# A decoder trunk in split float32: the down projection by seven block products instead of eight, and a scheduler that prices a port conflict

## The chip, the cores and the metric

The kernel runs on one core of one Trainium2 chip. Engines are named as in the profile: PE is TensorE (matmul), PEld its weight load, DVE is VectorE, ACT is ScalarE, POOL is GpSimd, SP is SyncE, which issues the DMAs. The metric is the device time of one execution in microseconds (us), lower being better.

## The reference

Two layers over 512 tokens of width 1024, all in float32. Each layer has a mixing part (four groups of attention heads that share an input projection and an output projection), then a squared-ReLU MLP, then a gated embedding added to the residual. The part that matters here:

```python
h = rmsnorm(x, g_pre_mlp)
m = jnp.square(jax.nn.relu(h @ w_up)) @ w_down   # 512x1024 @ 1024x4096, 512x4096 @ 4096x1024
x = x + rmsnorm(m, g_post_mlp)
x = x + jax.nn.sigmoid(x @ w_ple_gate) * (p_i @ w_ple_proj)
```

## The kernel before

**Arithmetic.** Every float32 operand of a large product is split into a high part `hi`, rounded to the type fp32r, and a rest `lo = x - hi`. `mm3` (L466) makes one product of 128 x 128 by 128 x 512 out of three matmuls: hi by hi, hi by lo, lo by hi. A split is one copy (`copy_r`, L461: ScalarE or VectorE) and one subtraction (`split`, L473: VectorE, or GpSimd where no operand lies in PSUM). Weights come by `wload` (L448): a DMA of 512 KB into a tile `wst` (2 buffers), then the split into `whi` and `wlo` (5 buffers each).

**Order of work.** The kernel is first recorded as a list of operations and then ordered by a planner (`schedule`, L290). It simulates the five engines with a price for each operation (`price`, L246) and a delay for each handover between engines (`SEEN`, L113), and takes on each engine the ready operation that was recorded first. The order that comes out is fixed: each engine runs its list in order. Operations recorded with `either` may go to one of two engines; `sooner_elsewhere` (L399) drops an engine if the operation would end sooner on the other, after adding a bias per engine (`plan.bias`). A buffer of a tag is handed out in the order of recording, to the next tile of the tag once all readers of an older one are done. The planner lets VectorE and GpSimd work side by side at full speed.

**The MLP** (`layer`, L1040). `up_tile(f)` (L1115) makes one of 32 tiles of the hidden activations, 128 hidden units by 512 tokens: 24 matmuls (8 steps of depth by 3) into a bank `ps_sc`, relu on ScalarE, a multiplication of that by the bank on VectorE, and the split into two scratch tiles. `down(g)` (L1130) multiplies 8 of these tiles by their weights through `token_major` (L1193): for each half of the 1024 columns four `wload` tiles and four banks (two `ps_mm`, two `ps_tp`), one for each 128 tokens, 192 matmuls in all. The four results are drained, the first group by a copy and the others by an addition to the accumulators `y`. In the fourth group the drained tile is also squared and summed, multiplied by a gain, normed, added to `x`, transposed on TensorE and split into `hT` for the gate product that follows. The loop is

```python
for g in range(5):
    for f in range(8):
        if g < 4:
            up_tile(8 * g + f)
        if g and f == 1:
            down(g - 1)
```

so that up tiles and down groups alternate on TensorE. A layer's MLP has 768 matmuls in the up and 768 in the down projection, each of 512 columns. `scratch` (L1187) takes its tiles in rotation from 20 buffers of the tags V, R and P0; the tag Z has 6 buffers, two of which hold the post gain during the MLP. PSUM has 8 banks: two `ps_mm`, two `ps_tp`, four `ps_sc`.

Of the kernel before, what the change touches and what calls it, by code (L numbers as in the profile page):

```python
# [134 lines left out]
class Plan:  # L135
# [110 lines left out]
    def price(self, eng, fn, a, k, outs, ins):  # L246
# [25 lines left out]
            return (470.0 if k.get("op") == ALU.pow else n * 2.1 + 147), 0.0  # L272
        return n * 0.833 + 244, 0.0

    @contextmanager
    def after(self, i):

        old, self.held = self.held, i
        yield
        self.held = old  # L280
# [9 lines left out]
    def schedule(self):  # L290
# [8 lines left out]
        now = dict.fromkeys(engines, 0.0)  # L299
        future = {e: [] for e in engines}  # L300
        avail = {e: [] for e in engines}
        dma, now["SP"] = 0.0, 560.0
        table = None
        waiting, live, last, queue = {}, {}, {}, {}

        def push(i):
            for e, r in ops[i].ready.items():
# [34 lines left out]
        while True:  # L342
            best = None
            for e in engines:
                f, v = future[e], avail[e]
                while f and (f[0][0] <= now[e] or ops[f[0][2]].done):
                    _, p, i = heapq.heappop(f)
                    heapq.heappush(v, (p, i))
                while v and ops[v[0][1]].done:
                    heapq.heappop(v)  # L350
                s = now[e] if v else f[0][0] if f else None
                if s is not None and (best is None or s < best[0]):
                    best = (s, e)
            if best is None:
                break
            s, e = best
            now[e] = max(now[e], s)
            f, v = future[e], avail[e]
            while f and f[0][0] <= s:
                _, p, i = heapq.heappop(f)  # L360
                heapq.heappush(v, (p, i))
            _, i = heapq.heappop(v)
            o = ops[i]
            if o.done or self.sooner_elsewhere(o, e, s, now, avail):
                continue
            o.start, o.done = s, True
            if o.alts:
                o.eng = e
                o.fn, o.a, o.k, o.cost, o.size = o.open[e]
            cost = o.cost  # L370
            if e == "PE" and s < COLD:
                cost *= 2
            if e == "ACT" and o.table and o.table != table:
                cost, table = cost + 1283, o.table
            now[e] = s + cost
            if e == "SP":
                dma = max(dma, s + cost + 650) + o.size
                o.end = dma
            else:
                o.end = now[e]  # L380
            order.append(i)
            for j in o.succ:
                q = ops[j]
                q.left -= 1
                after(q, e, o.end)
                if q.left == 0:
                    push(j)
            for t in o.tiles:
# [7 lines left out]
        self.total = max(o.end for o in ops)  # L396
        return order

    def sooner_elsewhere(self, o, e, s, now, avail):  # L399
        if not o.open or len(o.open) < 2:  # L400
            return False
        best = None
        for g, c in o.open.items():
            t = s if g == e else max(now[g], o.ready[g])
            if g != e:
                t += sum(self.ops[i].cost for p, i in avail[g] if p < o.prio and not self.ops[i].done
                         and not self.ops[i].alts)
            t += c[3] + o.bias.get(g, 0.0)
            if best is None or t < best[0]:
                best = (t, g)  # L410
        if best[1] != e:
            del o.open[e]
            del o.ready[e]
            return True
        return False
# [25 lines left out]
class Builder:  # L441
# [6 lines left out]
    def wload(self, src, S):  # L448

        nc = self.nc  # L450
        st = self.tile([128, 1024], F32, "wst")
        nc.sync.dma_start(st[:, :S], src)
        hi = self.tile([128, 1024], F32R, "whi")
        lo = self.tile([128, 1024], F32R, "wlo")
        s, h, l = st[:, :S], hi[:, :S], lo[:, :S]
        self.copy_r(h, s)
        self.plan.either(("vector", "tensor_tensor", (l, s, h.bitcast(F32)), dict(op=ALU.subtract)),
                         ("gpsimd", "tensor_tensor", (l, s, h.bitcast(F32)), dict(op=ALU.subtract)))
        return hi, lo

    def copy_r(self, out, src):  # L461

# [577 lines left out]
    def layer(self, L, x, last):  # L1040
        nc, t = self.nc, self.t
# [6 lines left out]
        with self.plan.shift(self.ple_shift):  # L1048
# [57 lines left out]
        self.token_major(lambda half, i: t["wo"][L, half, self.mixed[i]], [2 * g + k for g in self.mixed for k in (0, 1)],  # L1106
                         lambda k: (self.mixh[:, k, :], self.mixl[:, k, :]), evac_w, done_w, (False, True), part)

        self.plan.bias = {"DVE": self.mlp_bias}

        gpost2 = self.gain(t["g4"][L])
        xT = None
        uts = {}

        def up_tile(f):  # L1115
            wh, wl = self.wload(t["wu"][L, f], 1024)
            ps = self.tile([128, T], F32, "ps_sc")
            cs = (slice(0, 256), slice(256, 512)) if f < self.cut else (slice(0, 512),)
            for c in cs:
                for k in range(8):  # L1120
                    ks = slice(k * 128, (k + 1) * 128)
                    self.mm3(ps[:, c], wh[:, ks], wl[:, ks], hT[0][:, k, c], hT[1][:, k, c],
                             k == 0 and c == cs[0], k == 7 and c == cs[-1])
            r = self.tile([128, T], F32, "Z")
            nc.scalar.activation(r, ps, AF.Relu)
            nc.vector.tensor_tensor(r, r, ps, op=ALU.mult)
            uts[f] = (self.scratch(), self.scratch())
            self.split(*uts[f], r, sbuf=True)

        def down(g):  # L1130
            def evac_d(half, tt, ps):
                o = y[tt][half]
                if g == 0:
                    self.copy_r(o, ps)
                else:
                    nc.vector.tensor_tensor(o, ps, o, op=ALU.add)
                if g == 3:
                    self.square_half(ss2[tt], o, half, eps4[tt])
                    self.plan.either(*[(e, "tensor_tensor", (o, o, gpost2[half]), dict(op=ALU.mult))
                                       for e in ("gpsimd", "vector")])  # L1140

            def done_d(tt):
                nonlocal xT
                if g == 3:
                    if xT is None:
                        xT = self.new_hT()
                    self.add_normed(ss2[tt], y[tt], x[tt])
                    for i in range(2):
                        self.to_hT(x[tt][i], i, tt, xT)

            self.token_major(lambda half, i: t["wd"][L, g, half, i], range(8),
                             lambda k: uts[8 * g + k], evac_d, done_d, (False, g == 3))

        ss2 = [self.tile([128, 4], F32, "ss4") for tt in range(4)]
        for g in range(5):
            for f in range(8):
                if g < 4:
                    up_tile(8 * g + f)
                if g and f == 1:
                    down(g - 1)  # L1160


        self.plan.bias = {"DVE": 0.0 if last else self.mlp_bias}
# [23 lines left out]
    def scratch(self, dt=F32R):  # L1187

        self.unit += 1
        tags = ("V",) * 10 + ("R",) * 6 + ("P0",) * self.bufs[1]  # L1190
        return self.tile([128, T], dt, tags[self.unit * 7 % len(tags)])

    def token_major(self, src, korder, parts, evac, done, outer, part={}, fine=False):  # L1193
# [73 lines left out]
    first = ("v", "g", "v", "vg", "vg", "vg", "g", "g")  # L1267
    warm = 28

    parted = (0,)  # L1270
    part_tags = ("R", "V")

# [27 lines left out]
def _layout(inp):  # L1300

    f = lambda n: np.ascontiguousarray(np.asarray(inp[n]))
    w = f("w_in")
# [30 lines left out]
    a["wo"] = hv(f("w_out"), 2)  # L1334
    wu = f("w_mlp_up")
    a["wu"] = np.concatenate([chunks(wu[:, :, i * 128:(i + 1) * 128], 8) for i in range(32)], axis=1)
    wd = f("w_mlp_down").reshape(DEPTH, 4, 1024, D)
    a["wd"] = np.stack([hv(wd[:, g], 2) for g in range(4)], axis=1)
    a["wg"] = hv(f("w_ple_gate"), 2)
    a["wp"] = hv(f("w_ple_proj"), 2)[:, :, 0]  # L1340
    a["bf"] = f("b_forget")
# [26 lines left out]
```

## Time and profile before

| | us |
|---|---|
| median of 3 runs | 1509.18 (1507.07 to 1511.28) |
| the profiled execution, its own time | 1507.25 |
| its span, first to last instruction | 1505.5 |
| PE busy | 1445.8 (96%) |
| DVE busy | 908.8 (60%) |
| ACT busy | 661.1 (44%) |
| POOL busy | 376.7 (25%) |
| granted TensorE clock, mean over the span | 0.987 |

The time of the execution is 1.75 us more than its span. Busy time of PE is modelled: a matmul of 512 columns is listed with some 390 ns, and the next starts before that is over, so PE can be busy throughout and still have its pace set by the distance between starts. In time the kernel falls into mixing of layer 0 (to about 345 us), its MLP (to about 725), mixing of layer 1 (to about 1095) and its MLP (to about 1460); the gate product ends each layer.

### The profile page before, as it was taken

What the parts mean: (1) busy time and instruction counts of PE and PEld (TensorE: products, weight loads), DVE (VectorE), ACT (ScalarE), POOL (GpSimd) and SP (SyncE); (2) the same over time, 40 slices, a digit from 0 to 9 for tenths busy, and PEclk for the clock granted to TensorE, in tenths of its full rate; (3) what the DMA queues carried; (4) which work ended last, traced back from release to release, by engine and by line L of the source; (5) the groups of instructions that cost most, each with busy time, mean ns of one, the idle gap of its engine ahead of it and who ended that gap; (6) DMA issues with size and microseconds to landing.
All of it is one profiled execution on the core that took longest, in us unless ns stands there. A gap on an engine that the chain in (4) does not pass through costs nothing. (4 is left out here: it accounts for less than half of the span.)

```text
span 1505.5 us, 19889 instructions
## 1 busy us (share of the span) xinstructions
PE 1445.8 (96%) x7476; PEld 1173.3 (78%) x7476; DVE 908.8 (60%) x1789; ACT 661.1 (44%) x1299; POOL 376.7 (25%) x291
## 2 busy tenths in 40 slices
PE   6999998999999999999999999889999999999998
PEld 6967776778888888887789678577788888888877
DVE  7689998756424333335666999986553243433463
ACT  4266656745323223233344665666543341322321
POOL 5564556342000000002145636563310000000020
PEclk8899999999999999999999999999999999999999
DMA  4321122223222222221332211123132222222221
GB/s 160 100 86 57 57 78 98 78 84 112 99 90 93 98 98 88 94 98 56 122 118 71 74 55 64 64 64 120 52 131 98 99 88 94 98 98 90 92 77 63
DMA packets 44624, 133.91 MB, mean 89 GB/s; under 512 B 6896, under 2 KB 8176, under 8 KB 44528
## 3 DMA queue, kind: packets, MB, share of 16 engines
q1 hardware_dynamic: 44528, 132.64, 26.7%
q8 instruction: 59, 0.97, 0.3%
q14 instruction: 37, 0.30, 0.1%
HBM read 127.38 MB, written 5.24 MB: 88 GB/s over the span
## 5 line engine op out<-in xcount | busy, mean ns | idle before, releaser
L429 DVE TENSOR_TENSOR wlo<-wst,whi 128x1024 fp32r<-128x1024 f32 x150 | 184.2, 1228 | 355.6 <-ACT whi L429 355.4
L429 ACT ACTIVATE whi<-wst 128x1024 fp32r<-128x1024 f32 (+1 forms) x212 | 222.7, 1051 | 397.0 <-PE ps_tp L429 202.1
L429 POOL TENSOR_TENSOR wlo<-wst,whi 128x1024 fp32r<-128x1024 f32 (+1 forms) x70 | 168.5, 2410 | 164.2 <-ACT whi L429 155.8
L429 PE MATMUL ps_sc<-htl,whi 128*128 128x512 f32 (+1 forms) x544 | 208.5, 384 | 1.1 <-DVE htl L429 1.1
L429 PE MATMUL ps_sc<-hth,whi 128*128 128x512 f32 (+1 forms) x544 | 207.6, 383 | 0.3 <-ACT hth L429 0.3
L429 PE MATMUL ps_sc<-hth,wlo 128*128 128x512 f32 (+1 forms) x544 | 206.5, 380 | 0.0
L429 POOL TENSOR_SCALAR ss<-ss,eps 128x1 f32<-128x1 f32 x8 | 3.7, 473 | 637.1 <-ACT Z L429 637.1
L429 PE MATMUL ps_mm<-hth,whi 128*128 128x512 f32 (+1 forms) x400 | 148.3, 372 | 9.6 <-DVE R L429 9.2
L429 PE MATMUL ps_mm<-htl,whi 128*128 128x512 f32 (+1 forms) x400 | 148.1, 371 | 1.8 <-DVE htl L429 1.8
L429 PE MATMUL ps_mm<-hth,wlo 128*128 128x512 f32 (+1 forms) x400 | 146.2, 366 | 0.0
L429 PE MATMUL ps_mm<-whi,htl 128*128 128x512 f32 (+2 forms) x344 | 121.1, 353 | 5.6 <-DVE htl L429 5.6
L429 PE MATMUL ps_mm<-whi,hth 128*128 128x512 f32 (+2 forms) x344 | 122.0, 355 | 0.3 <-DVE V L429 0.2
L429 PE MATMUL ps_mm<-wlo,hth 128*128 128x512 f32 (+2 forms) x344 | 120.1, 350 | 0.1
L429 PEld LDWEIGHTS ps_sc<-hth,whi 128*128 128x128 f32 x544 | 102.0, 188 | 23.0 <-ACT hth L429 0.5
L429 PEld LDWEIGHTS ps_sc<-htl,whi 128*128 128x128 f32 x544 | 102.2, 188 | 22.4 <-DVE htl L429 1.5
L429 PEld LDWEIGHTS ps_sc<-hth,wlo 128*128 128x128 f32 x544 | 102.3, 188 | 21.9
L429 ACT ACTIVATE Z<-Z,m 128x256 f32<-128x256 f32 (+3 forms) x160 | 86.2, 541 | 39.4 <-DVE m L429 38.7
L429 PE MATMUL ps_tp<-whi,V 128*128 128x512 f32 x256 | 96.4, 394 | 0.0
L429 PE MATMUL ps_mm<-whi,V 128*128 128x512 f32 x256 | 96.4, 394 | 0.0
L429 PEld LDWEIGHTS ps_mm<-hth,whi 128*128 128x128 f32 x400 | 77.8, 195 | 20.6 <-issue 11.5
L429 POOL TENSOR_TENSOR R<-R,R 128x512 fp32r<-128x512 f32 (+1 forms) x58 | 76.6, 1321 | 59.1 <-ACT R L429 46.0
L429 PEld LDWEIGHTS ps_mm<-htl,whi 128*128 128x128 f32 x400 | 78.0, 195 | 13.1 <-issue 3.0
(213 smaller groups left out, 2957.4 us busy)
## 6 DMA issues: line engine op xcount, KB each, us to landing
wst<-in_wu SPq DMA_DIRECT2D x64, 512.0 KB, 3.2
wst<-in_wd SPq DMA_DIRECT2D x64, 512.0 KB, 3.2
wst<-in_wq SPq DMA_DIRECT2D x40, 512.0 KB, 3.5
wst<-in_wo SPq DMA_DIRECT2D x16, 512.0 KB, 3.3
wst<-in_wg SPq DMA_DIRECT2D x16, 512.0 KB, 3.2
R<-in_x SPq DMA_DIRECT2D x16, 256.0 KB, 3.6
Z<-in_g SPq DMA_DIRECT2D x16, 256.0 KB, 3.6
wst<-in_wv SPq DMA_DIRECT2D x8, 512.0 KB, 3.2
```

What stands on the lines that cost most here:

```text
L429: r = getattr(getattr(nc, eng), fn)(*[res(v) for v in o.a], **{n: res(v) for n, v in o.k.items()})
```

## The change

The down projection of the first 24 of the 32 hidden tiles is taken in 4 groups (`groups = 4`) of 3 pairs of tiles. A pair is a depth of 2 x 128; with two halves of the tokens (256 each) and two halves of the columns (512 each), it is a product of 2 x 2 by 2 x 2 blocks. Seven block products stand for the eight, with sums and differences of blocks on both sides (`sums` for the activations, the first loop of `down` and its second for the weights), and sums of the products over all pairs kept in `acc` and combined once (`blocks`). The last 8 tiles go the old way (`down_rest`).

```diff
-            r = self.tile([128, T], F32, "Z")
+            r = us[f] = self.tile([128, T], F32, "Z")
             nc.scalar.activation(r, ps, AF.Relu)
-            nc.vector.tensor_tensor(r, r, ps, op=ALU.mult)
-            uts[f] = (self.scratch(), self.scratch())
-            self.split(*uts[f], r, sbuf=True)
+            nc.scalar.activation(r, r, AF.Square)
+            if f >= 6 * self.groups:
+                uts[f] = (self.scratch(), self.scratch())
+                self.split(*uts[f], r, sbuf=True)
+            elif f % 2:
+                sums(f // 2)
+        def sums(p):
+            a, b = us.pop(2 * p), us.pop(2 * p + 1)
+            z = self.tile([128, T], F32, "Z")
+            y4 = self.tile([128, 256], F32, "Z")
+            self.either(ALU.add, z[:, lt], a[:, rt], b[:, rt])
+            self.either(ALU.subtract, z[:, rt], z[:, lt], a[:, lt])
+            self.either(ALU.subtract, a[:, rt], a[:, lt], a[:, rt])
+            self.either(ALU.subtract, y4, b[:, lt], z[:, rt])
+            for src, left, right in ((a, 1, 7), (z, 5, 6), (b, 2, 4), (y4, 3, None)):
...
         def down(g):
+            pairs = range(3 * g, 3 * g + 3)
+            banks = {n: [self.tile([128, T], F32, tag) for i in range(2)]
+                     for n, tag in (("x", "ps_mm"), ("y", "ps_tp"), ("v", "ps_sc"), ("w", "ps_sc"))}
+            for p in pairs:
+                a = self.tile([128, 1024], F32, "wst")
+                b22, t1 = self.scratch(F32), self.scratch(F32)
+                t2 = T2[p] = self.scratch(F32)
+                nc.sync.dma_start(a, t["wd"][L, 2 * p])
+                nc.sync.dma_start(b22, t["wd"][L, 2 * p + 1, :, 512:])
+                self.either(ALU.subtract, t1, a[:, w2], a[:, w1])
+                self.either(ALU.subtract, t2, b22, t1)
+                self.either(ALU.subtract, a[:, w2], b22, a[:, w2])
+                h, l = self.wparts()
+                self.split(h, l, a, sbuf=True)
+                B[p, 1], B[p, 7] = (h[:, w1], l[:, w1]), (h[:, w2], l[:, w2])
+                h, l = self.wparts()
+                for src, w, i in ((t1, w1, 5), (t2, w2, 6)):
+                    self.split(h[:, w], l[:, w], src, sbuf=True)
...
+            for p in pairs:
+                for n, bank in ((1, "x"), (5, "v"), (7, "w"), (6, "y")):
+                    for i in range(2):
+                        product(p, n, bank, i, p == pairs[0], p == pairs[-1])
+            for n, bank in ((1, "x"), (5, "v"), (7, "w"), (6, "y")):
+                for i in range(2):
+                    add(acc[n][i], banks[bank][i], g == 0)
+            for p in pairs:
+                c = self.tile([128, 1024], F32, "wst")
+                nc.sync.dma_start(c, t["wd"][L, 2 * p + 1])
+                self.either(ALU.subtract, T2[p], c[:, w1], T2[p])
...             # split of c for products 2 and 3, split of T2 for product 4,
...             # products 2 (bank x), 3 (v), 4 (w) of the three pairs, drained like the first four
+        def blocks():
+            for i in range(2):
+                a = {n: acc[n][i] for n in acc}
+                for o, b in ((2, 1), (6, 1), (5, 6), (3, 5), (5, 7), (4, 7), (4, 6)):
+                    self.either(ALU.add, a[o], a[o], a[b])
+        for f in range(32):
+            up_tile(f)
+            if f and f % 6 == 0 and f <= 6 * self.groups:
+                down(f // 6 - 1)
+                if f == 6 * self.groups:
+                    blocks()
+        down_rest()
```

In `down_rest` the multiplication by the gain goes to VectorE alone, where the planner chose before. The biases of the MLP up to there become 1000 ns for VectorE and 4000 ns for GpSimd (before: 500 and 0). `scratch` rotates over 29 buffers: 10 of V, 11 of R, 4 of P0 and the 4 of `tab`, which hold the rope tables during the mixing. The numbers of buffers of each tag stay.

The planner gets a model of a port that VectorE and GpSimd share. It acts on the whole kernel, not on the MLP alone:

```diff
+    def shared(self, fn, a):
+        ins = [v for v in a[1:] if isinstance(v, View) and v.free() > 64]
+        if any(self.psum(v) for v in a if isinstance(v, View)):
+            return False
+        return len(ins) > 1 or fn[1] in ("tensor_copy", "tensor_scalar")
...
+            if e == "DVE" and self.shared(o.fn, o.a):
+                cost += max(0.0, port["POOL"] - s)
+                port["DVE"] = s + cost
+            if e == "POOL":
+                cost += max(0.0, port["DVE"] - s)
+                port["POOL"] = s + cost
```

`sooner_elsewhere` counts the same: an engine that would have to wait for the port is priced from the time when the port comes free.

## Rows read from the trace of the kernel before

**Rows 1.** Page, part 2: the span in 40 slices, busy tenths of each engine.
```profile
PE   6999998999999999999999999889999999999998
DVE  7689998756424333335666999986553243433463
PEclk8899999999999999999999999999999999999999
```

**Rows 2.** Busy time by stretch: both MLPs, the end of one, both mixing stages.
```profile
core 0: us, PE busy (x) PEld busy (x) DVE busy (x) ACT busy (x) POOL busy (x), PEclk, DMA share, GB/s
375.00:694.00 319.00, 319.00 (x1374) 257.72 (x1373) 122.02 (x138) 99.97 (x132) 4.36 (x6) 1.00 0.28 94
1100.00:1430.00 330.00, 329.93 (x1435) 267.46 (x1436) 128.59 (x147) 105.93 (x139) 4.54 (x6) 1.00 0.29 96
694.00:735.00 41.00, 35.08 (x159) 27.70 (x158) 25.03 (x29) 13.87 (x23) 9.79 (x10) 0.96 0.17 58
...
25.00:300.00 275.00, 251.83 (x1583) 203.62 (x1582) 240.06 (x631) 161.31 (x385) 141.05 (x84) 0.97 0.25 79
780.00:1040.00 260.00, 245.93 (x1557) 197.65 (x1556) 227.57 (x607) 157.43 (x380) 135.48 (x80) 0.99 0.22 71
```

**Rows 3.** Chain that ended last, in order of time: start us, us, step.
```profile
1193.36 44.80 PE ps_sc L429 x192
...
1371.72 33.57 PE ps_sc L429 x144
```

**Rows 4.** Groups of instructions by shape, VectorE: count, busy us, mean ns, idle before.
```profile
L429 DVE TENSOR_TENSOR wlo<-wst,whi 128x1024 fp32r<-128x1024 f32 x150 | 184.2, 1228 | 355.6 <-ACT whi L429 355.4
L429 DVE TENSOR_TENSOR Z<-Z,ps_sc 128x512 f32<-128x512 f32 x64 | 43.5, 680 | 0.0
...
L429 DVE TENSOR_TENSOR P<-ps_tp,P 128x256 fp32r<-128x256 f32 x48 | 19.1, 415 | 0.5 <-ACT P L429 0.5
L429 DVE TENSOR_TENSOR P<-ps_mm,P 128x512 f32<-128x512 f32 x24 | 16.5, 688 | 12.1 <-PE ps_mm L429 12.1
...
L429 DVE TENSOR_TENSOR R<-Z,V 128x512 fp32r<-128x512 f32 x18 | 12.5, 693 | 12.6 <-ACT V L429 12.6
```

**Rows 5.** The same for ScalarE.
```profile
L429 ACT ACTIVATE whi<-wst 128x1024 fp32r<-128x1024 f32 x204 | 215.8, 1059 | 386.0 <-PE ps_tp L429 202.1 <-PE ps_sc L429 146.9 <-PE ps_mm L429 17.8
L429 ACT ACTIVATE Z<-ps_sc 128x512 f32<-128x512 f32 x64 | 37.1, 580 | 0.0
...
L429 ACT ACTIVATE V<-Z 128x512 fp32r<-128x512 f32 x32 | 20.2, 632 | 43.8 <-DVE Z L429 43.8
...
L429 ACT ACTIVATE P<-ps_tp 128x256 fp32r<-128x256 f32 x40 | 14.6, 375 | 4.6 <-PE ps_tp L429 4.5
```

**Rows 6.** Page, part 6, DMA issues: count, KB each, us from issue to landing.
```profile
wst<-in_wd SPq DMA_DIRECT2D x64, 512.0 KB, 3.2
```

**Rows 7.** Timeline of GpSimd and of VectorE, layer 0 mixing: start us, us, instruction.
```profile
109.22 2.37 POOL L429 TENSOR_TENSOR wlo<-wst,whi 128x1024 fp32r<-128x1024 f32 x1 [0.45 <-ACT whi L429]
...
109.25 2.89 DVE L429 TENSOR_TENSOR R<-R,tab 128x512 f32<-128x512 f32 x1
```

**Rows 8.** Groups of VectorE instructions with two SBUF inputs, used in the mixing stages.
```profile
L429 DVE TENSOR_TENSOR R<-R,tab 128x512 f32<-128x512 f32 x13 | 19.7, 1517 | 0.2
...
L429 DVE TENSOR_TENSOR R<-R,R 128x512 f32<-128x512 f32 x11 | 15.1, 1372 | 0.2
...
L429 DVE TENSOR_TENSOR htl<-O,hth 128x512 fp32r<-128x512 f32 x8 | 12.4, 1566 | 0.1
```

**Rows 9.** Timeline at the end of layer 0's MLP: VectorE, GpSimd, TensorE.
```profile
703.01 1.42 DVE L429 SCALAR_TENSOR_TENSOR R<-P,ss,R 128x512 f32<-128x512 f32 x2 [0.80 <-POOL ss L429]
...
719.29 3.50 DVE L429 SCALAR_TENSOR_TENSOR R<-P,ss,R 128x512 f32<-128x512 f32 x2 [0.80 <-POOL ss L429]
...
719.22 2.35 POOL L429 TENSOR_TENSOR wlo<-wst,whi 128x1024 fp32r<-128x1024 f32 x1
...
722.27 1.04 PE L429 MATMUL ps_sc<-ident,R 128*128 128x128 f32 x4 [2.55 <-DVE R L429]
```

More of the change, by code (lines that the diff above doesn't have):

```diff
@@ L304, in schedule @@
         waiting, live, last, queue = {}, {}, {}, {}
+        port = {"DVE": 0.0, "POOL": 0.0}
         def push(i):
@@ L363, in schedule @@
             o = ops[i]
-            if o.done or self.sooner_elsewhere(o, e, s, now, avail):
+            if o.done or self.sooner_elsewhere(o, e, s, now, avail, port):
                 continue
@@ L397, in schedule, with sooner_elsewhere @@
         return order
-    def sooner_elsewhere(self, o, e, s, now, avail):
+    def sooner_elsewhere(self, o, e, s, now, avail, port):
         if not o.open or len(o.open) < 2:
@@ L407, in sooner_elsewhere @@
                          and not self.ops[i].alts)
+            if g == "POOL" or g == "DVE" and self.shared(c[0], c[1]):
+                t = max(t, port["DVE" if g == "POOL" else "POOL"])
             t += c[3] + o.bias.get(g, 0.0)
@@ L451, in wload, with wparts, either @@
         st = self.tile([128, 1024], F32, "wst")
[L452 to L458, printed above, removed]
+        for i, part in enumerate(src if isinstance(src, list) else [src]):
+            n = S // len(src) if isinstance(src, list) else S
+            nc.sync.dma_start(st[:, i * n:(i + 1) * n], part)
+        hi, lo = self.wparts()
+        self.split(hi[:, :S], lo[:, :S], st[:, :S], sbuf=True)
         return hi, lo
+    def wparts(self):
+        return self.tile([128, 1024], F32R, "whi"), self.tile([128, 1024], F32R, "wlo")
+    def either(self, op, out, a, b):
+        self.plan.either(*[(e, "tensor_tensor", (out, a, b), dict(op=op)) for e in ("vector", "gpsimd")])
     def copy_r(self, out, src):
@@ L1107, in layer @@
                          lambda k: (self.mixh[:, k, :], self.mixl[:, k, :]), evac_w, done_w, (False, True), part)
-        self.plan.bias = {"DVE": self.mlp_bias}
+        self.plan.bias = {"DVE": 1000.0, "POOL": 4000.0}
         gpost2 = self.gain(t["g4"][L])
         xT = None
-        uts = {}
+        us, parts, uts = {}, {}, {}
+        lt, rt = slice(0, 256), slice(256, 512)
+        w1, w2 = slice(0, 512), slice(512, 1024)
         def up_tile(f):
@@ L1123, in up_tile @@
                              k == 0 and c == cs[0], k == 7 and c == cs[-1])
-            r = self.tile([128, T], F32, "Z")
+            r = us[f] = self.tile([128, T], F32, "Z")
             nc.scalar.activation(r, ps, AF.Relu)
-            nc.vector.tensor_tensor(r, r, ps, op=ALU.mult)
-            uts[f] = (self.scratch(), self.scratch())
-            self.split(*uts[f], r, sbuf=True)
-        def down(g):
-            def evac_d(half, tt, ps):
-                o = y[tt][half]
-                if g == 0:
+            nc.scalar.activation(r, r, AF.Square)
@@ new lines, in up_tile @@
+            if f >= 6 * self.groups:
[11 more added lines that the diff above has]
+            self.either(ALU.subtract, y4, b[:, lt], z[:, rt])
+            q = parts[p] = {}
+            for src, left, right in ((a, 1, 7), (z, 5, 6), (b, 2, 4), (y4, 3, None)):
+                n = src.free()
+                hi, lo = self.scratch(), self.scratch()
+                self.split(hi[:, :n], lo[:, :n], src, sbuf=True)
+                q[left] = hi[:, lt], lo[:, lt]
+                q[right] = hi[:, rt], lo[:, rt]
@@ new lines, in down, with product, add @@
+        def down(g):
+            pairs = range(3 * g, 3 * g + 3)
+            banks = {n: [self.tile([128, T], F32, tag) for i in range(2)]
+                     for n, tag in (("x", "ps_mm"), ("y", "ps_tp"), ("v", "ps_sc"), ("w", "ps_sc"))}
+            B, T2 = {}, {}
+            for p in pairs:
[13 more added lines that the diff above has]
+                    self.split(h[:, w], l[:, w], src, sbuf=True)
+                    B[p, i] = h[:, w], l[:, w]
+            def product(p, n, bank, i, start, stop):
+                c = slice(i * 128, (i + 1) * 128)
+                ah, al = parts[p][n]
+                self.mm3(banks[bank][i], ah[:, c], al[:, c], *B[p, n], start, stop)
+            def add(o, ps, first):
+                if first:
@@ L1136, in evac_d @@
                     nc.vector.tensor_tensor(o, ps, o, op=ALU.add)
[L1137 to L1140, printed above, removed]
+            for p in pairs:
+                for n, bank in ((1, "x"), (5, "v"), (7, "w"), (6, "y")):
+                    for i in range(2):
+                        product(p, n, bank, i, p == pairs[0], p == pairs[-1])
@@ new lines, in down @@
+            for n, bank in ((1, "x"), (5, "v"), (7, "w"), (6, "y")):
[5 more added lines that the diff above has]
+                self.either(ALU.subtract, T2[p], c[:, w1], T2[p])
+                h, l = self.wparts()
+                self.split(h, l, c, sbuf=True)
+                B[p, 2], B[p, 3] = (h[:, w1], l[:, w1]), (h[:, w2], l[:, w2])
+                h, l = self.wparts()
+                self.split(h[:, w1], l[:, w1], T2[p], sbuf=True)
+                B[p, 4] = h[:, w1], l[:, w1]
@@ new lines, in down @@
+            for p in pairs:
+                for n, bank in ((3, "v"), (4, "w"), (2, "x")) if p == pairs[-1] else ((2, "x"), (3, "v"), (4, "w")):
+                    for i in range(2):
+                        product(p, n, bank, i, p == pairs[0], p == pairs[-1])
+            for n, bank in ((3, "v"), (4, "w"), (2, "x")):
+                for i in range(2):
+                    add(acc[n][i], banks[bank][i], g == 0)
+        def blocks():
+            for i in range(2):
+                a = {n: acc[n][i] for n in acc}
+                for o, b in ((2, 1), (6, 1), (5, 6), (3, 5), (5, 7), (4, 7), (4, 6)):
+                    self.either(ALU.add, a[o], a[o], a[b])
@@ L1142, in done_d, with down_rest, evac_d @@
+        def down_rest():
+            def evac_d(half, tt, ps):
+                o = y[tt][half]
+                nc.vector.tensor_tensor(o, ps, o, op=ALU.add)
+                self.square_half(ss2[tt], o, half, eps4[tt])
+                nc.vector.tensor_tensor(o, o, gpost2[half], op=ALU.mult)
             def done_d(tt):
                 nonlocal xT
[L1144 to L1149, printed above, removed]
@@ L1151, in down @@
-            self.token_major(lambda half, i: t["wd"][L, g, half, i], range(8),
-                             lambda k: uts[8 * g + k], evac_d, done_d, (False, g == 3))
-        ss2 = [self.tile([128, 4], F32, "ss4") for tt in range(4)]
[L1155 to L1160, printed above, removed]
+                if xT is None:
+                    xT = self.new_hT()
@@ new lines, in done_d @@
+                self.add_normed(ss2[tt], y[tt], x[tt])
+                for i in range(2):
+                    self.to_hT(x[tt][i], i, tt, xT)
+            f0 = 6 * self.groups
+            self.token_major(lambda half, i: [t["wd"][L, f0 + 2 * i + j, :, 512 * half:512 * half + 512] for j in range(2)],
+                             range(8), lambda k: uts[f0 + k], evac_d, done_d, (False, True))
+        acc = {2: [y[0][0], y[1][0]], 3: [y[0][1], y[1][1]], 4: [y[2][0], y[3][0]], 5: [y[2][1], y[3][1]]}
@@ L1163, in layer @@
+        a7 = self.tile([128, 1024], F32, "S")
+        acc[7] = a7[:, w1], a7[:, w2]
+        for n in (1, 6):
+            acc[n] = [self.tile([128, T], F32, "X") for i in range(2)]
+        ss2 = [self.tile([128, 4], F32, "ss4") for tt in range(4)]
+        for f in range(32):
[5 more added lines that the diff above has]
+        down_rest()
         self.plan.bias = {"DVE": 0.0 if last else self.mlp_bias}
@@ L1189, in scratch @@
         self.unit += 1
-        tags = ("V",) * 10 + ("R",) * 6 + ("P0",) * self.bufs[1]
+        tags = ("V",) * 10 + ("R",) * 11 + ("P0",) * self.bufs[1] + ("tab",) * 4
         return self.tile([128, T], dt, tags[self.unit * 7 % len(tags)])
@@ L1268 @@
     warm = 28
+    groups = 4
     parted = (0,)
@@ L1336, in _layout @@
     a["wu"] = np.concatenate([chunks(wu[:, :, i * 128:(i + 1) * 128], 8) for i in range(32)], axis=1)
-    wd = f("w_mlp_down").reshape(DEPTH, 4, 1024, D)
-    a["wd"] = np.stack([hv(wd[:, g], 2) for g in range(4)], axis=1)
+    a["wd"] = f("w_mlp_down").reshape(DEPTH, 32, 128, D)
     a["wg"] = hv(f("w_ple_gate"), 2)
```

## The prediction

> **What bounds the kernel now.** I read the slices first. TensorE is near full almost everywhere, VectorE is full only in the mixing stages and under half in the MLPs, where the clock is granted in full [rows 1]. Then the stretches: over 319 us of layer 0's MLP TensorE is busy for all 319.00, VectorE for 122.02, ScalarE for 99.97 and GpSimd for 4.36; over 330 us of layer 1's it is 329.93 against 128.59, 105.93 and 4.54 [rows 2]. So the MLP is bound by TensorE alone, and GpSimd is as good as out of it already: "no GpSimd in the MLP" says what must not come back when VectorE gets more to do. Busy time of pipelined matmuls can hide their pace, so I take that from the chain of waits, which runs through TensorE without a gap there: 192 matmuls in 44.80 us and 144 in 33.57 [rows 3], 233.2 ns each. That is the price of a matmul that goes. The end of an MLP is another matter: TensorE works 35.08 of 41 us [rows 2] and waits up to 2.55 us at a time for VectorE [rows 9]. In the mixing stages VectorE is the fuller of the other engines, busy 240.06 of 275 and 227.57 of 260 us, with GpSimd busy for over half [rows 2].
>
> **What goes.** A pair cost 2 x 8 x 3 = 48 matmuls (two steps of depth, eight blocks of 128 x 512, three each). Now it costs seven products of two 128-token tiles, three each: 42. Twelve pairs in each of two layers: 12 x 2 x 6 = 144 matmuls, and 144 x 0.2332 = **33.6 us**. All matmuls keep their 512 columns, and nothing is added on TensorE.
>
> **What is added, and whether it is covered.** One group is 6 up tiles and 3 pairs, on TensorE 144 + 126 = 270 matmuls, 63.0 us, of which the pairs take 29.4.
> VectorE, down part, for a pair: four subtractions on weights at 0.693 (the 128x512 row R<-Z,V), 2.8; low parts of two 1024-wide tiles at 1.228 and of three 512-wide at 0.693, 4.5; three pairs 21.9; 14 drains at 0.688, 9.6; together 31.5 us [rows 4]. Up part: six low parts of weights at 1.228, 7.4; for a pair four half-width sums and one half-width low part at 0.415 (the nearest row, one operand in PSUM) and three at 0.693, 4.2, three times 12.5; together 19.8 [rows 4]. Sum 51.3 of 63.0 us, or 81%.
> ScalarE: six copies of weights at 1.059, 6.4; relu at 0.580 and square at 0.632 (nearest row, V<-Z) for six tiles, 7.3; high parts of a pair 3 x 0.632 + 0.375 on the activations and 2 x 1.059 + 3 x 0.632 on the weights, 18.9 for three; together 32.6 of 63.0 [rows 5]. Both fit, so on the average the added work lies beside TensorE and costs nothing. The multiplication by the bank that leaves VectorE, 0.680 a tile [rows 4], is counted as gone.
>
> **Where it need not fit.** In the pairs alone VectorE has 31.5 us of work against TensorE's 29.4, so weights must be prepared ahead, during the up tiles, and what allows that is buffers. A group asks for 24 scratch tiles of activations and 9 for weights, 33 out of 29. Followed through the rotation, the tile that comes short is the same in every group: b22 of the third pair. Its buffer comes free when the first pair's products 1, 5 and 7 are done, 18 matmuls or 4.2 us into the group. From there: DMA 3.2 [rows 6], two subtractions 1.4, the copy 1.06, the low part 1.23 [rows 4, 5] and about 0.5 for handovers: ready at 11.6 us. TensorE gets to the third pair after 48 matmuls, at 11.2. Late by 0.4 at best, and by 1.6 if a 1.23 us instruction is in front on VectorE; product 5, which needs no b22 and takes 1.4 us, may go first and cover it. So 0 to 1.6 us a group; I take 0.7, near the middle, eight groups: **5.6 us lost**, with 0 and 13 as ends. On SP that load waits in a fixed queue, with the first weights of the second pass behind it; these are due at 16.8 us (72 matmuls) and need 3.2 + 0.7 + 1.1 + 1.2 + 0.5 = 6.7 us, so they may be issued as late as 10.
> Other waits that are new: the second pass writes the banks of the first after they are drained. Bank x is finished 18 matmuls, 4.2 us, before it is written again and two drains take 1.4 us; the next up tile's bank is v, finished 12 matmuls before it is asked for. Both fit. Z has four buffers beside the gain, and a pair takes just four (two activations, z and y4); they come back about 8 us after the second tile, from the relu, square, four sums and splits above, while a pair takes 11.2 us. Sums in `blocks`, 14 at 0.693 = 9.7 us, lie under seven up tiles of 5.6 us each. The split of wd's reads adds bytes (2560 columns a pair for 2048), and DMA is busy 0.28 of the time in the MLP [rows 2].
>
> **End of the MLP.** In layer 0 two of the normed additions to x take 3.50 us where two others take 1.42, because a GpSimd subtraction of 2.35 us started just before; TensorE waits 2.55 us for it [rows 9], and this occurs twice there. With a price on the port the planner may keep these apart, but it looks at the port at the moment of choosing, and the subtraction comes first. Ends: 0 and the two waits, 5.1 us. I take **2 us won**.
>
> **The mixing stages.** The port model reorders them. In rows 7 a VectorE multiplication of two SBUF tiles takes 2.89 us beside a GpSimd subtraction of 2.37 that began 0.03 us earlier. Against 0.693 clean, three kinds of VectorE instruction lose 19.7 - 13 x 0.693 = 10.7, 15.1 - 11 x 0.693 = 7.5 and 12.4 - 8 x 0.693 = 6.9 us: 25 us over both layers [rows 4, 8]. The planner did not see this; now it does, and each choice between the engines shifts. At best all 25 us return, at worst about as many are lost, when operations move from GpSimd to a VectorE that is 87% busy [rows 2]. I take **0**, the middle. The new scratch rotation also gives two tiles of the embedding's input buffers of P0 and tab, which come free late in the mixing; counted in the same range.
>
> **Sum.** Profiled execution 1507.25 - 33.6 + 5.6 - 2 + 0 = 1477.3. The median of the runs shown is 1.9 above that execution, within their spread of 4.2, so I forecast **1479** for a median.
>
> **Rivals.**
> *Port conflicts return their time (faster).* VectorE is the fuller partner in the mixing stages and the conflict is serial [rows 2, 7]; if the planner avoids half of the 25 us and VectorE sets the pace, 1479 - 12 = 1467. For it: TensorE is busy only 251.83 of 275 us there. Against: a planner that chooses operation by operation doesn't see the conflict that it causes a moment later. The Trainium skill (SBUF — State Buffer, "Who interferes with whom") has this as a rule: a VectorE instruction with two SBUF inputs and a GpSimd instruction that reads SBUF exclude each other for the whole of an instruction, whichever began first. By that rule, the trace agrees (2.89 us for 0.693), and counting the conflict is right.
> *The reordering hurts the mixing.* Same place, other sign: half of 25 us moved onto VectorE without return, 1479 + 12 = 1491.
> *VectorE sets the pace of the pairs (slower).* A pair's weights go through one chain: DMA 3.2, subtraction of the block and of its neighbour 1.4, copy 1.06, low part 1.23, handovers 0.6, 7.5 us, where TensorE needs 24 matmuls, 5.6 us, for the first pass [rows 3 to 6]. If buffers let the planner work only one pair ahead, each of 24 pairs is late by 1.9 us: 46 us lost for 33.6 won, 1479 - 5.6 + 46 = 1519. It decides from 1.4 us a pair. For it: VectorE's 31.5 us in 29.4. Against: two wst and five whi buffers let two pairs be prepared at a time, and the up tiles give 33.6 us in which VectorE has 19.8 us to do.
> *GpSimd stays in the MLP.* The bias of 4000 ns only makes it dear; once VectorE's queue is longer than that, the planner uses it and VectorE's two-input instructions stand still for up to 2.35 us each time [rows 9]. With one in every group 8 x 2.35 = 19 us if nothing covers it: 1498.
>
> **How the numbers follow.** Forecast 0.55 (1472 to 1487 by its own ends), faster rival 0.18, mixing hurt 0.11, GpSimd stays 0.04, VectorE's pace 0.08, and 0.04 for a mixture that cancels out. What a measurement of this kernel can tell from no change is 0.3%, 4.5 us: faster is below 1504.7. The first four cases are faster, 0.88, less 0.04 for their upper tails; same 0.06, slower 0.10. The range runs from 1459, where the faster rival returns more than half, to 1503, which leaves out the last two cases and little else.
>
> **What would show it.** TensorE: 7332 matmuls for 7476, still 233 ns apart in the pairs, no wait for VectorE or ScalarE over 2 us in a group, and the span from the first up tile to the gate product some 14 us shorter in each layer. VectorE near 80% in the MLPs, ScalarE near 50%, GpSimd near zero. If the groups show repeated waits of over 4 us for wlo or whi, the rival on VectorE's pace is right; if the time outside the MLPs moves by more than 10 us, the part on the mixing was wrong.

## Result, and the profile after

The changed kernel takes 1459.46 us (median of 4 runs, 1457.08 to 1461.01) against 1508.12 for the kernel before, a ratio of 0.9674 with a 95% interval of 0.9652 to 0.9697. It is faster by 48.7 us, where I had forecast 30; the time lies at the lower end of my range.

Cut where TensorE starts the first up tile and the gate product of a layer (start times of these matmuls in the traces), the span falls into five stretches. The last four columns are kernels of the experiments below.

| us | before | after | port alone | no port | late split | late, no port |
|---|---|---|---|---|---|---|
| mixing, layer 0 | 350.3 | 341.4 | 341.6 | 350.7 | 342.0 | 349.5 |
| MLP, layer 0 | 365.8 | 353.7 | 362.6 | 356.2 | 345.8 | 350.4 |
| gate product and mixing, layer 1 | 374.1 | 362.7 | 361.0 | 373.4 | 360.6 | 373.0 |
| MLP, layer 1 | 364.8 | 350.6 | 362.8 | 351.5 | 345.0 | 346.8 |
| gate product, layer 1 | 50.5 | 50.7 | 50.6 | 50.6 | 50.7 | 50.5 |
| span | 1505.5 | 1459.2 | 1478.5 | 1482.4 | 1444.1 | 1470.2 |

So 26.3 us came from the MLPs and 20.2 from the mixing stages, on which I had put 30 and 0.

The page's slices after; they answer to [rows 1]. VectorE is now mostly at 5 to 8 tenths in the MLPs (3 to 5 in the slices at their ends), and TensorE is at 9 in nearly every slice.

```profile
PE   6999999999999999999999999999999999999998
...
DVE  7679999757666766845766899987575677777373
```

Busy time by stretch after: the two mixing stages, then the two MLPs (us, PE, PEld, DVE, ACT, POOL busy with counts, clock, DMA share, GB/s).

```profile
0.00:341.00 341.00, 318.64 (x1923) 259.25 (x1924) 272.23 (x712) 205.46 (x473) 157.65 (x122) 0.96 0.27 87
695.00:1058.00 363.00, 353.78 (x2107) 287.36 (x2106) 287.18 (x707) 214.89 (x486) 161.76 (x120) 0.99 0.27 87
341.00:695.00 354.00, 347.04 (x1539) 280.60 (x1538) 233.63 (x342) 171.43 (x260) 11.46 (x16) 1.00 0.32 106
1058.00:1408.00 350.00, 344.02 (x1535) 278.75 (x1534) 232.44 (x341) 170.64 (x258) 12.05 (x16) 1.00 0.32 106
```

The same view of the kernel before, its mixing stages cut at its own matmuls:

```profile
0.00:350.00 350.00, 319.84 (x1923) 260.11 (x1924) 284.87 (x707) 201.65 (x472) 175.99 (x129) 0.96 0.27 86
716.00:1090.00 374.00, 355.73 (x2097) 287.07 (x2097) 296.45 (x700) 212.15 (x486) 168.22 (x121) 0.99 0.25 80
```

In the mixing TensorE has the matmuls that it had and is as busy. VectorE executes a few instructions more (712 and 707 for 707 and 700) and is busy for 12.6 + 9.3 = 21.9 us less. It is the same work with less standing still: the groups of [rows 8] after are

```profile
L446 DVE TENSOR_TENSOR R<-R,R 128x512 f32<-128x512 f32 x12 | 12.5, 1044 | 0.2
L446 DVE TENSOR_TENSOR R<-R,tab 128x512 f32<-128x512 f32 x12 | 12.3, 1026 | 1.4 <-POOL tab L446 1.2
...
L446 DVE TENSOR_TENSOR htl<-O,hth 128x512 fp32r<-128x512 f32 x8 | 6.5, 828 | 2.6 <-ACT hth L446 2.5
```

Over their clean 0.693 us each these three kinds lose 4.2 + 4.0 + 1.0 = 9.2 us, where they lost 25.0.

In the MLPs the matmuls stay 0.233 us apart (33.51 us for 144, to be set beside [rows 3]):

```profile
414.05 33.51 PE ps_sc L446 x144
```

TensorE's waits in layer 0's MLP after (us in total, times, longest):

```profile
PE ps_mm L446 <- DVE wlo L446: 1.8, 1, 1.8
PE ps_sc L446 <- ACT hth L446: 1.8, 1, 1.8
PE ps_sc L446 <- DVE wlo L446: 1.4, 1, 1.4
PE ps_sc L446 <- DVE htl L446: 0.9, 1, 0.9
PE ps_tp L446 <- ACT whi L446: 0.7, 1, 0.7
PE ps_mm L446 <- ACT whi L446: 0.3, 1, 0.3
```

The two for the split of `hT` stand at the start of the MLP (349.9 and 351.3 us). All others stand between 579 and 617 us, in and just behind the fourth group of pairs, and the same waits stand at that place in layer 1. Counted as distance between starts beyond 0.233 us, this place loses 7.9 us in layer 0 and 4.9 in layer 1 (an expectation below has 7.4 and 5.9; the sum is nearly the same). Part of layer 0's is not a wait: behind 2 us with TensorE busy for 1.53 and 2 us with it busy for 0.60 the granted clock is 0.50, the lower of its two levels (1.2 of 2.4 GHz), and the matmuls stand 0.42 us apart, which makes some 1.5 us. In layer 1 the clock stays at 1.00 there.

```profile
592.00:594.00 2.00, 1.53 (x5) 0.56 (x3) 2.00 (x4) 0.00 (x0) 0.00 (x0) 1.00 0.00 0
594.00:596.00 2.00, 0.60 (x2) 0.52 (x3) 2.00 (x4) 0.00 (x0) 0.00 (x0) 0.84 0.00 0
596.00:598.00 2.00, 2.00 (x6) 1.63 (x5) 2.00 (x3) 0.63 (x1) 0.00 (x0) 0.50 0.69 254
```

The first three groups have no wait over 0.1 us.

### The profile page after: what moved, and what is told of

Read it like the earlier page. It is cut to its first block, busy times and chain, and to the rows that moved or that the text cites. A ratio compares the mean times of both kernels' runs of the same rounds, so it can differ in the third digit from the quotient of the medians.

```text
span 1459.2 us, 20200 instructions
## 1 busy us (share of the span) xinstructions
PE 1410.5 (97%) x7332; PEld 1145.1 (78%) x7332; DVE 1051.5 (72%) x2132; ACT 775.8 (53%) x1496; POOL 345.8 (24%) x275
## 4 chain that ended last, share of the span: by engine, by line
PE 71%; DVE 20%; DMA 3%; ACT 3%; issue 2%; POOL 1%; SPq 0%; DVEq 0%; ACTq 0%; POOLq 0%
PE ps_sc L446 33%; PE ps_mm L446 25%; PE ps_tp L446 11%; DVE Z L446 4%; DVE P L446 4%; DVE S L446 3%; DVE m L446 2%; PE ps_sc L443 2%; DVE wlo L446 2%; DVE R L446 2%; DVE O L446 1%; ACT Z L446 1%; DMA wst<-in_wu 1%; DVE X L446 1%; DVE s L446 1%
## 5 line engine op out<-in xcount | busy, mean ns | idle before, releaser
L446 ACT ACTIVATE whi<-wst 128x1024 fp32r<-128x1024 f32 (+1 forms) x217 | 228.1, 1052 | 212.5 <-DMA wst<-in_wu 62.3
L446 DVE TENSOR_TENSOR wlo<-wst,whi 128x1024 fp32r<-128x1024 f32 x153 | 187.3, 1227 | 118.1 <-ACT whi L446 118.0
L446 POOL TENSOR_TENSOR wlo<-wst,whi 128x1024 fp32r<-128x1024 f32 (+1 forms) x67 | 158.8, 2375 | 180.9 <-ACT whi L446 171.9
L446 POOL TENSOR_SCALAR ss<-ss,eps 128x1 f32<-128x1 f32 x8 | 6.8, 866 | 644.2 <-ACT Z L446 644.2
L446 PE MATMUL ps_mm<-htl,whi 128*128 128x512 f32 (+1 forms) x400 | 144.8, 362 | 0.1
L446 PEld LDWEIGHTS ps_mm<-hth,wlo 128*128 128x128 f32 x400 | 76.8, 192 | 11.0 <-issue 2.7
L446 POOL TENSOR_TENSOR R<-R,R 128x512 fp32r<-128x512 f32 (+1 forms) x56 | 72.1, 1289 | 50.6 <-ACT R L446 46.2
L446 PEld LDWEIGHTS ps_mm<-whi,hth 128*128 128x128 f32 x344 | 66.7, 194 | 8.8 <-issue 1.7
```

Source lines behind the costliest of these rows:

```text
L446: r = getattr(getattr(nc, eng), fn)(*[res(v) for v in o.a], **{n: res(v) for n, v in o.k.items()})
```

## Experiments

Every kernel was timed beside the kernel before; the ratio is to that one.

**Which part of the change shortened the mixing?** Three kernels: the port model alone, everything but the port model, and the new rotation of scratch tiles alone.

```diff
 # port_alone, to the kernel before: shared(), port in schedule() and in sooner_elsewhere(), as in the change
 # no_port, to the changed kernel: these lines taken out of schedule() and sooner_elsewhere()
 # rotation_alone, to the kernel before:
-        tags = ("V",) * 10 + ("R",) * 6 + ("P0",) * self.bufs[1]
+        tags = ("V",) * 10 + ("R",) * 11 + ("P0",) * self.bufs[1] + ("tab",) * 4
```

> The kernel before with the port model in the planner and nothing else of the change. Theory (the 20 us that the time outside the MLPs lost come from the port model): 16 to 20 us shorter than before, 1488 to 1492, nearly all of it between the first instruction and the first up tile of layer 0 and between the gate product of layer 0 and the first up tile of layer 1; VectorE's time held in two-input instructions there falls from 62 us to about 26. A few us more are possible at the ends of the MLPs, where the port is in play too. Rival (the mixing gained from the new rotation of scratch tiles, which moves the embedding's tiles to other buffers, or from what the MLP leaves behind): within 4 us of before, 1504 to 1512.

Measured: 1480.51 us against 1509.22, ratio 0.9823 (0.9804 to 0.9842). The mixing is 21.8 us shorter (20.2 in the changed kernel), and the MLPs 3.2 and 2.1. The rows of its two mixing stages have VectorE's busy time of the changed kernel:

```profile
0.00:341.00 341.00, 318.66 (x1922) 259.38 (x1923) 271.58 (x712) 205.57 (x473) 157.60 (x122) 0.96 0.27 88
704.00:1065.00 361.00, 350.77 (x2106) 284.80 (x2105) 286.96 (x706) 215.69 (x487) 162.59 (x120) 1.00 0.26 84
```

The whole is 28.7 us, more than the 16 to 20 that I gave: the "few us more" at the ends of the MLPs are 5.3, and the mixing gives 21.8. Over all VectorE instructions that the planner calls shared, with a clean length linear in the columns through 0.693 us at 512 and 1.228 at 1024 (0.74 at 512 for those with two operations), the time beyond it in the mixing falls from some 62 to some 28 us. At the ends of the MLPs TensorE of the kernel before loses 3.9 and 2.5 us between starts to waits for VectorE's `R`; with the port model alone these waits are gone.

> The changed kernel without the port model: the block products, the new rotation and the new biases stay, the planner again lets VectorE and GpSimd work side by side at full speed. Theory (port model): the mixing stages are back at their old length, 20 us longer than in the changed kernel, about 1480; the MLPs stay near 353 and 351 us. Rival (rotation or the MLP): within 4 us of 1459. A second rival, that the two parts of the change need each other: more than 1490, because GpSimd comes back into the MLP.

Measured: 1485.18 us against 1509.22, ratio 0.9848 (0.9828 to 0.9869). The mixing is back at 350.7 and 373.4 us, and the three groups of [rows 8] read as before, as here the one on the rope tables:

```profile
L438 DVE TENSOR_TENSOR R<-R,tab 128x512 f32<-128x512 f32 x13 | 19.7, 1518 | 0.2
```

The MLPs stay near the changed kernel's. Of the 5 us that this is above my 1480 the traces show 3.4 in the MLPs; the mixing stages are 20.0 us longer than in the changed kernel, as expected. The two parts of the change don't need each other.

> The kernel before with the new rotation of scratch tiles (29 buffers for 20) and nothing else. Theory (port model): within 4 us of before, 1504 to 1512. Rival (rotation): 10 to 20 us shorter.

Measured: 1508.84 us against 1509.22, ratio 0.9998 (0.9988 to 1.0009). The rotation does nothing by itself.

**Why does TensorE wait in the fourth group, and only there?** The trace of the changed kernel there: SP's issues (the first is for the second group), VectorE, TensorE (start us, us; idle before).

```profile
411.36 0.38 SPq L446 DMA_DIRECT2D V<-in_wd  x1
...
576.91 0.33 SPq L446 DMA_DIRECT2D R<-in_wd  x1
...
579.75 0.69 DVE L446 TENSOR_TENSOR V<-R,P 128x512 f32<-128x512 f32 x1 [0.53 <-DMA R<-in_wd]
580.36 0.68 DVE L446 TENSOR_TENSOR wst<-R,wst 128x512 f32<-128x512 f32 x1
...
582.29 1.22 DVE L446 TENSOR_TENSOR wlo<-wst,whi 128x1024 fp32r<-128x1024 f32 x1
...
581.16 0.73 PE L446 MATMUL ps_tp<-whi,V 128*128 128x512 f32 x2 [0.68 <-ACT whi L446]
...
595.39 0.80 PE L446 MATMUL ps_mm<-wlo,R 128*128 128x512 f32 x1 [1.83 <-DVE wlo L446]
```

The six up tiles in front of the group are 144 matmuls in 33.55 us from 539.41 in the chain of waits, so the group starts at about 573.0 and the second pair is due 5.6 us later, at 578.6. Its b22 (`R<-in_wd`) is issued at 576.91, 3.9 us into the group, and the split of what hangs on it ends at 583.5. In the second group the second pair's b22 (`V<-in_wd`) was issued at 411.36, 36 us ahead of that group. What the issue waited for stands in the chain that ended last: it follows at once on 12 matmuls into `ps_sc`, the first pair's products 5 and 7.

```profile
539.41 33.55 PE ps_sc L446 x144
574.33 2.58 PE ps_sc L446 x12
576.91 2.82 DMA R<-in_wd
```

The code says why it is this group: up tile 24 is recorded before `down(3)` and is the first that takes its two scratch tiles at once, so the fourth group asks for 24 + 2 + 9 = 35 tiles and not 33, and it is the second pair that comes short.

```diff
 # late_split, to the changed kernel (split_up is the split of one tile into its two scratch tiles)
-            if f >= 6 * self.groups:
-                uts[f] = (self.scratch(), self.scratch())
-                self.split(*uts[f], r, sbuf=True)
+            if f > 6 * self.groups:
+                split_up(f)
...
                 if f == 6 * self.groups:
+                    split_up(f)
                     blocks()
```

> The changed kernel, with one statement moved: the split of hidden tile 24 into its two scratch tiles is recorded after the fourth group of pairs and not before it, so the fourth group asks for 33 scratch tiles like the other three and not for 35. Theory (TensorE's waits in the fourth group, 7.4 us in layer 0 and 5.9 in layer 1, come from weights that wait for a scratch buffer, and the other three groups show that 33 tiles are few enough): the waits go, 10 to 13 us less than the changed kernel, 1446 to 1450. Rival (the fourth group waits because VectorE has the most to do there, with the sums of blocks behind it): the waits stay, within 4 us of 1459.

Measured: 1445.58 us against 1509.22, ratio 0.9581 (0.9565 to 0.9598), 13.9 us less than the changed kernel, a little more than I gave, which makes it the fastest of all. The traces have 7.9 and 5.6 us of it in the two MLPs. Between its MLPs' starts and ends TensorE waits for nothing but the split of `hT`; layer 0:

```profile
PE ps_sc L446 <- ACT hth L446: 1.7, 1, 1.7
PE ps_sc L446 <- DVE htl L446: 0.9, 1, 0.9
```

while VectorE has the same to do as before the edit (its row of that MLP; the changed kernel has 233.63):

```profile
342.00:688.00 346.00, 343.43 (x1538) 279.85 (x1537) 233.20 (x341) 171.47 (x259) 11.90 (x16) 1.00 0.32 109
```

So neither the sums of blocks nor VectorE's load made the fourth group wait by itself.

**The same shortage in every group.**

```diff
 # late_27, to late_split
-        tags = ("V",) * 10 + ("R",) * 11 + ("P0",) * self.bufs[1] + ("tab",) * 4
+        tags = ("V",) * 10 + ("R",) * 9 + ("P0",) * self.bufs[1] + ("tab",) * 4
```

> The changed kernel with the late split of tile 24, and with 27 buffers in the rotation of scratch tiles for 29 (two of R fewer), so that every group is as short as the fourth was in the changed kernel: 33 tiles out of 27 for 35 out of 29. Theory (the waits come from a load that waits for a scratch buffer): followed through the rotation, b22 of the second pair comes free 4 us into the first, third and fourth group, as in the changed kernel's fourth, and in time in the second; three groups with 6 to 7.5 us of waits in each layer, 36 to 45 us over the late split, 1482 to 1490, and no waits in the second group. Rival (the fourth group was slow for its sums or for VectorE's load): within 6 us of 1445.6.

Measured: 1466.99 us against 1508.42, ratio 0.9720 (0.9702 to 0.9738), 21.4 us over the late split. The place is as expected: waits in the first and the third group, as here the third's, and none over 0.1 us in the second.

```profile
524.62 0.73 PE L446 MATMUL ps_tp<-whi,R 128*128 128x512 f32 x2 [1.14 <-ACT whi L446]
525.65 0.73 PE L446 MATMUL ps_mm<-whi,V 128*128 128x512 f32 x2 [0.30 <-ACT whi L446]
537.16 0.50 PE L446 MATMUL ps_mm<-wlo,tab 128*128 128x512 f32 x1 [0.53 <-DVE wlo L446]
```

The size is half of what I gave or less: 3.5 and 2.8 us for these groups in layer 0, and behind the fourth only 1.7, where I had put 6 to 7.5 in each. Layer 1 has 3.4, 2.9 and 1.7, so the waits make 16.0 of the 21.4 us. Another 1.6 are a stretch at the start of layer 0's MLP with a granted clock of 0.59 (354 to 358 us), and the mixing stages are 4.0 us longer, for which I have no cause. The buffer explains that there are waits and in which groups; why they are this long is open, and I did not work out what the planner finds to put in front.

**The block products by themselves.** `late_no_port` is `no_port` with the late split.

> The kernel before with the block products (with the late split of tile 24), the new rotation and the new biases, and without the port model. If 144 matmuls at 0.2332 us are what the block products give once no buffer is short, 33.6 us less than before: 1473 to 1478, and each MLP 16 to 18 us shorter than before. If the products cost something elsewhere, that shows as a smaller gain; if the port model is needed for them, as a much smaller one.

Measured: 1472.85 us against 1508.42, ratio 0.9765 (0.9746 to 0.9784), 35.6 us less than before; the MLPs are 15.4 and 18.0 us shorter, the first a little less than I gave. This is the 33.6 us of the 144 matmuls, within the scatter of the runs. With the port model alone at 28.7 the two add up to 64.3; together they give 1509.22 - 1445.58 = 63.6.

**Order or choice?** The port model has two halves, the longer time of an operation that meets the other engine (order), and the choice of the engine.

```diff
 # port_order_only, to port_alone
-            if g == "POOL" or g == "DVE" and self.shared(c[0], c[1]):
-                t = max(t, port["DVE" if g == "POOL" else "POOL"])
 # port_choice_only, to port_alone (and the same for POOL)
-                cost += max(0.0, port["POOL"] - s)
-                port["DVE"] = s + cost
+                port["DVE"] = s + cost + max(0.0, port["POOL"] - s)
```

> The kernel before with one half of the port model: an operation that meets the other engine on the port is simulated as longer, but the choice between VectorE and GpSimd doesn't look at the port. Theory A (the 28.7 us of the whole port model come from a truer order: work that waits for a held operation is no longer put in front of work that could run): most of it, 1480 to 1490. Theory B (they come from choosing the other engine while the port is taken): little, 1500 to 1510.

Measured: 1490.40 us against 1508.40, ratio 0.9885 (0.9867 to 0.9903).

> The other half: the planner keeps account of when the port comes free and counts it in the choice between VectorE and GpSimd, but simulates each operation at its old length. Theory A (truer order): little, 1500 to 1510. Theory B (choice of the engine): most of it, 1480 to 1490.

Measured: 1494.90 us against 1508.40, ratio 0.9914 (0.9900 to 0.9927). Neither theory holds alone: 18.0 us from the order, 13.5 from the choice, 31.5 together and 28.7 in one kernel. The traces go with it: by a count like the one above, which gives 64 us for the kernel before, VectorE is held in the mixing for 48 us with the order alone and 50 with the choice alone.

**What do the other edits in the MLP give?** The biases back to 500 and 0, and the squaring back on VectorE, each on the late split.

```diff
 # late_old_bias
-        self.plan.bias = {"DVE": 1000.0, "POOL": 4000.0}
+        self.plan.bias = {"DVE": self.mlp_bias}
 # late_square_dve
-            nc.scalar.activation(r, r, AF.Square)
+            nc.vector.tensor_tensor(r, r, ps, op=ALU.mult)
```

> The changed kernel with the late split of tile 24, and with the biases of the MLP as before (500 for VectorE, 0 for GpSimd for 1000 and 4000). If the new biases are what keeps GpSimd out and this matters, GpSimd is busy for tens of us in each MLP, VectorE is held beside it, and the time is 5 to 20 us above the late split's 1445.6. If TensorE sets the pace with room to spare, GpSimd may come back and the time stays within 4 us of 1445.6.

Measured: 1447.02 us against 1508.40, ratio 0.9591 (0.9578 to 0.9604). GpSimd is back, busy for 62.70 of 240 us of layer 0's MLP beside VectorE, and TensorE doesn't notice. The late split's row comes first:

```profile
400.00:640.00 240.00, 240.00 (x1035) 194.05 (x1034) 170.10 (x250) 122.56 (x177) 0.00 (x0) 1.00 0.35 119
400.00:640.00 240.00, 240.00 (x1036) 194.10 (x1035) 174.29 (x207) 115.59 (x165) 62.70 (x54) 1.00 0.36 119
```

> The changed kernel with the late split of tile 24, and with the squaring of the relu on VectorE as before (a multiplication by the bank, 0.68 us) for ScalarE's 0.63. VectorE is then busy for 64 x 0.68 = 43 us more, some 79% in the MLPs for 71%. If TensorE sets the pace with room to spare: within 4 us of 1445.6. If VectorE's work is near the limit in the groups: 5 us or more above, as waits of TensorE for wlo.

Measured: 1448.19 us against 1508.40, ratio 0.9598 (0.9584 to 0.9611). VectorE is busy for 183.13 us of the same stretch (170.10 in the late split), and again TensorE is full:

```profile
400.00:640.00 240.00, 240.00 (x1035) 193.92 (x1034) 183.13 (x273) 108.18 (x155) 0.00 (x0) 1.00 0.36 118
```

Both stand within 3 us of the late split, and their intervals overlap its own. "Relu-square on ScalarE, no GpSimd in the MLP" is worth nothing that these runs can tell, once no buffer is short.

## Why the prediction was too small

**The step that failed is "The mixing stages. [...] I take 0, the middle".** The bounds, 25 us either way, held; the value between them was wrong by 20.2 us. I set against the gain a loss from "when operations move from GpSimd to a VectorE that is 87% busy". Few moved: VectorE has 12 instructions more in both mixing stages together, GpSimd 8 fewer. And VectorE's time there did not rise by it; it went down, by 21.9 us in the changed kernel, whose mixing got 20.2 us shorter, and by 22.8 in the one with the port model alone, whose mixing got 21.8 shorter. What changed is when the operations run and, for a few, on which engine. The rival "port conflicts return their time" was the right mechanism with too small a price: I put half of the 25 us of three kinds of instruction, where all kinds together were held for some 62 us, and with the port model some 34 of these came back. The Trainium skill (SBUF — State Buffer, "Who interferes with whom") says that a VectorE instruction with two SBUF inputs and a GpSimd one that reads SBUF exclude each other for the whole of an instruction, the first comer winning. The traces agree (2.89 us for 0.693 in [rows 7]). The wait is real time on VectorE, so a planner that leaves it out is wrong by it each time. I had the row and the rule and still gave them only a rival's 0.18 and nothing in the sum.

**What goes** was right: 33.6 us worked out, 35.6 measured for the block products with no buffer short, 33.4 of them in the MLPs.

**Where it need not fit** was right in kind and wrong in place. I followed the rotation with 33 tiles for every group and overlooked the two of up tile 24. The loss was to be 5.6 us over eight groups, with 13 as the far end. It is 13.9, in and behind the two fourth groups, and the other six, which I had charged with 0.7 us each, have no wait over 0.1 us. The third pair's b22 comes as late as I had it there (issued 4.3 to 4.4 us into each of layer 0's first three groups, for my 4.2), and product 5 or other work covers it. Of the other waits that I checked (banks, Z, the sums of blocks, DMA), TensorE shows none over 0.3 us.

**Whether it is covered** held: 81% of VectorE and 52% of ScalarE were worked out for a group. Two whole groups of the changed kernel show 73% and 50%, and layer 0's whole MLP 233.63 of 354 us (66%) and 171.43 (48%), the eight old-style tiles included. VectorE's price was too high because back to back its 512-wide instructions, listed with 0.69 us, start 0.61 us apart (579.75 and 580.36 us above).

```profile
413.90:539.40 125.50, 125.50 (x542) 101.51 (x541) 91.18 (x141) 62.40 (x91) 0.00 (x0) 1.00 0.33 109
```

The rival on VectorE's pace is refuted by the run that gives VectorE more to do and loses nothing, and that on GpSimd by the run that lets it back in.

**The end of the MLP**: 2 us won were forecast; the port model alone has 5.3 net in the MLPs, after what the start of an MLP loses by it (in layer 0 of that kernel TensorE waits 1.3 + 0.9 us there for the split of `hT`). My way there was not it: the two engines still meet at that place (last section), but TensorE no longer waits for it.

That the MLPs together came to 26.3 us where I had 30 is partly luck: about 8 us more than I gave were lost to the buffers, and about 4 us more were won by the port model.

## What to carry to other kernels

If two engines exclude each other, the price of it belongs in the model that orders the work: here that alone gave 28.7 us, not far below the 35.6 of a rewrite that saves 144 matmuls, and it was readable beforehand in the groups whose mean is far above their clean length. When a change needs buffers in a rotation, count the tiles between the first and the last use in the order of recording for every group, the last one included: two tiles more in one of four groups cost 13.9 us of the 35.6. With the bounding engine full and without waits, moving work between the others brought nothing that showed here.

## What the hardware showed beyond that

The conflict can lengthen a GpSimd instruction too, when that comes second. At the end of layer 0's MLP in the changed kernel a GpSimd subtraction begins 0.18 us after the first of two additions on VectorE and takes 2.82 us, where one that began ahead of such an addition took 2.35 [rows 9]; the second of the additions then waits for it, and the two take 3.55 us for the 1.41 of the pair before them. TensorE has other work there and waits for neither.

```profile
686.48 1.41 DVE L446 SCALAR_TENSOR_TENSOR R<-P,ss,R 128x512 f32<-128x512 f32 x2 [0.80 <-POOL ss L446]
...
693.52 3.55 DVE L446 SCALAR_TENSOR_TENSOR R<-P,ss,R 128x512 f32<-128x512 f32 x2
...
693.70 2.82 POOL L446 TENSOR_TENSOR wlo<-wst,whi 128x1024 fp32r<-128x1024 f32 x1 [0.82 <-ACT whi L446]
```
